# Second half of a 3-D average pool: contiguous loads read two rows at a time, and all stores behind the loads

## The chip, the cores and the metric

The kernel runs on one core of one Trainium2 chip. The metric is the device time of one execution in microseconds, taken as the median of several runs.

## The reference

The input x has the shape (8, 32, 32, 32, 32): batch, channels, depth, height, width, all in float32, 33.5 MB. The output is the mean of every 2 x 2 x 2 window of (depth, height, width), without overlap:

```python
for i, j, k over the output grid (16, 16, 16):
    window = x[:, :, 2*i:2*i+2, 2*j:2*j+2, 2*k:2*k+2]
    result[:, :, i, j, k] = np.mean(window, axis=(-3, -2, -1))
```

The output is float32, 4.2 MB. No element of x is used twice, so the kernel must read 33.5 MB and write 4.2 MB.

## The kernel before

Batch and channels together make 256 rows, each a volume of 32 x 32 x 32 floats, or 128 KB. The kernel takes the rows in two halves of 128, and each row of a half lies on one of the 128 partitions. In the code, `t` is the half and KF = 256 floats (1 KB) is the unit of length along a row: a row is 128 units of input and 16 units of output. One unit of output needs eight units of input, that is two depth slices.

The list `plan` sets the order: for each half, four tiles `tin` of 32 units (32 KB per partition, 4 MB in all) are loaded. The first six tiles are each loaded by one DMA of 4 MB. The last two tiles of the second half are loaded in two parts of 16 units each, 2 MB. In DRAM, neighbouring partitions of such a load lie 128 KB apart. All ten loads are issued by the queue of SyncE (SP) on line 77, in the order of the plan. The pool has five buffers, so the sixth load and the later ones wait until VectorE (DVE) is done with the tile that had the buffer before.

Each tile, or part of one, goes through `pool_unit` on VectorE: line 58 adds the two depth slices (half as many elements come out), line 62 adds neighbours along the width, line 65 adds neighbours along the height, scales by 1/8, and writes the result into `obuf`, one buffer of 16 KB per partition for each half. Line 65 appears in the profile as two instructions, the sum itself and a short one that reads an accumulator which nobody uses.

Four stores on line 92 take the results out, in units of 1 KB per partition: (half 1, units 0 to 1) on the queue of ScalarE (ACT), then on SP (half 0, all 16 units), (half 1, units 2 to 13), and (half 1, units 14 and 15). Since SP takes its instructions in order, its three stores are issued behind the tenth load; the one on ACT is issued as soon as its results are there.

The code after the pool works on the compiled program. It moves the first load in front of the barrier that opens the program, and it rewrites the end, so that SP waits for the stores' semaphores last and everything else is cleared before.

Of the kernel before, what the change touches and what calls it, by code (L numbers as in the profile page):

```python
# [1 line left out]

# [4 lines left out]

F32 = mybir.dt.float32
KF = 256


@with_exitstack
def pool_rows(
    ctx: ExitStack,
    tc: tile.TileContext,
    x: bass.AP,
    kernel_size: int,
    out: bass.AP,
):
    nc = tc.nc  # L20
    assert kernel_size == 2, "only kernel_size == 2 supported"

    B, C, D, H, W = x.shape
    P = nc.NUM_PARTITIONS
    assert (B * C, D, H, W) == (2 * P, 32, 32, 32)
    add = mybir.AluOpType.add

    xv = x.rearrange("b c d h w -> (b c) (d h w)")  # L30
    ov = out.rearrange("b c d h w -> (b c) (d h w)")

    pool_in = ctx.enter_context(tc.tile_pool(name="pin", bufs=5))
    pool_out = ctx.enter_context(tc.tile_pool(name="pout", bufs=1))
    obuf = [pool_out.tile([P, 16 * KF], F32, name=f"obuf{t}") for t in range(2)]
    dummy = pool_out.tile([P, 1], F32, name="dummy")


    plan = [
        (0, 0, (32,)),
        (0, 32, (32,)),
        (0, 64, (32,)),
        (0, 96, (32,)),
        (1, 0, (32,)),
        (1, 32, (32,)),
        (1, 64, (16, 16)),
        (1, 96, (16, 16)),  # L50
    ]

    def pool_unit(buf, t, k0, kb):

        od = kb // 8
        a = buf.rearrange("p (o dd e) -> p o dd e", o=od, dd=2)
        b = buf[:, :od * 1024]
        nc.vector.tensor_add(  # L58
            out=b.rearrange("p (o e) -> p o e", o=od), in0=a[:, :, 0], in1=a[:, :, 1])
        bv = b.rearrange("p (e ww) -> p e ww", ww=2)  # L60
        c = buf[:, od * 1024:od * 1536]
        nc.vector.tensor_add(out=c, in0=bv[:, :, 0], in1=bv[:, :, 1])  # L62
        cv = c.rearrange("p (j hh k) -> p j hh k", hh=2, k=16)
        o0 = k0 * KF // 8
        nc.vector.tensor_tensor_reduce(  # L65
            out=obuf[t][:, o0:o0 + od * 256].rearrange("p (j k) -> p j k", k=16),
            in0=cv[:, :, 0], in1=cv[:, :, 1],
            scale=0.125, scalar=0.0, op0=add, op1=add, accum_out=dummy[:, :],
        )

    for t, k0, parts in plan:
        tin = pool_in.tile([P, 32 * KF], F32, tag="tin", name="tin")
        views = []
        o = 0
        for kb in parts:
            v = tin[:, o * KF:(o + kb) * KF]
            nc.sync.dma_start(  # L77
                out=v, in_=xv[t * P:(t + 1) * P, (k0 + o) * KF:(k0 + o + kb) * KF])
            views.append((v, k0 + o, kb))
            o += kb  # L80
        for v, k, kb in views:
            pool_unit(v, t, k, kb)

    for queue, t, k0, kb in [
        (nc.scalar, 1, 0, 2),
        (nc.sync, 0, 0, 16),
        (nc.sync, 1, 2, 12),
        (nc.sync, 1, 14, 2),  # L90
    ]:
        queue.dma_start(
            out=ov[t * P:(t + 1) * P, k0 * KF:(k0 + kb) * KF],
            in_=obuf[t][:, k0 * KF:(k0 + kb) * KF],
        )


def kernel(tc: tile.TileContext, x: bass.AP, kernel_size: int, out: bass.AP):
    nc = tc.nc
    pool_rows(tc, x, kernel_size, out)  # L100
    tc.close()
    tc.compile()  # L102
    blocks = nc.main_func.blocks

    opening, program = blocks[0].instructions, blocks[tc.starting_block_idx].instructions
    load = next(i for i in program if isinstance(i, mybir.InstDMACopy))
    assert load.engine == nc.sync.engine
    barrier = next(  # L110
        n for n, i in enumerate(opening)
        if i.engine == load.engine and isinstance(i, mybir.InstDrain))
    program.remove(load)
    opening.insert(barrier, load)

    closing = blocks[-1].instructions
    stores = [  # L120
        i for i in program
        if isinstance(i, mybir.InstDMACopy) and "out_" in i.outs[0].memref]
    kept = [u.id for i in stores for u in i.sync_info.on_update]
    kept = [n for j, n in enumerate(kept) if n not in kept[j + 1:]]
    final = next(
        i for i in closing
        if i.engine == nc.sync.engine and isinstance(i, mybir.InstDrain))
    waits = {w.id: w for w in final.sync_info.on_wait}
    closing[closing.index(final)] = mybir.InstDrain(
        name=final.name, engine=final.engine, ins=[], outs=[], is_reset_sema=False,  # L130
        sync_info=mybir.SyncInfo(
            on_wait=[w for n, w in waits.items() if n not in kept], on_update=[]))


    reset = next(
        n for n, i in enumerate(closing)
        if isinstance(i, mybir.InstDrain) and i.is_reset_sema)
    first, stop = closing[reset].reset_range_start, closing[reset].reset_range_stop
    assert isinstance(closing[reset + 1], mybir.InstISA)
    while len(closing) > reset:  # L140
        closing.pop()
    n = first
    while n < stop:
        m = n
        while m < stop and m not in kept:
            m += 1
        if m > n:
            closing.append(mybir.InstDrain(
                name=nc.get_next_instruction_name(), engine=nc.gpsimd.engine, ins=[], outs=[],
                is_reset_sema=True, reset_range_start=n, reset_range_stop=m))  # L150
            nc.gpsimd.sem_clear(range(n, m))
        n = m + 1
    for n in kept:
        w = waits[n]
        closing.append(mybir.InstEventSemaphore(
            name=nc.get_next_instruction_name(), engine=nc.sync.engine, ins=[], outs=[],
            sync_info=mybir.SyncInfo(
                on_wait=[w],
                on_update=[mybir.SyncUpdate(
                    sync_type="semaphore", id=n, ant_name=w.ant_name,  # L160
                    update_mode="sem-sub-imm", update_value=w.wait_value)])))


# [1 line left out]
_INS = ['x', 'kernel_size']  # L165
_OUTS = [((8, 32, 16, 16, 16), 'float32')]

_NUMBERS = {'kernel_size': 2}


# [26 lines left out]
```

## Time and profile before

| | |
|---|---|
| median of 7 runs (lowest to highest) | 91.81 us (91.58 to 92.01) |
| the profiled execution's own time | 92.05 us |
| its span, first to last instruction | 86.8 us |
| VectorE busy | 64.1 us, 40 instructions |
| HBM read, written | 33.55 MB, 4.19 MB |
| share of DMA in the chain that ended last | 83% |

The span ends with the last instruction of VectorE and of the queues; a store that is still under way then is not part of it. The last store is issued at the span's end and takes 4.9 us to land, and the rest of the 92.05 us lies before the first and after the last thing that the trace shows.

In the page, a row of part 2 cuts the span into 40 slices: the digits are the mean busy share of the 16 DMA engines, in tenths. A row of a table of stretches gives a start and an end in microseconds, then its length, the busy time of VectorE and GpSimd in it, the clock, the share of the DMA engines and the GB/s that they moved. A packet is put down to the stretch that it starts in, so short stretches are rough.

### The profile page before, as it was taken

Reading aid. Unit: us, or ns where it says so; the run is one execution under the profiler, and the core shown is the slowest. Engines: PE = TensorE matmul, PEld = TensorE weight load, DVE = VectorE, ACT = ScalarE, POOL = GpSimd, SP = SyncE. Lnnn points to the kernel's source line nnn. Section 1 sums busy time; section 2 is a strip of 40 time slices with the busy share of each in tenths; the row PEclk is TensorE's granted clock in tenths of the full one; section 3 lists DMA queues with packets and bytes.
Section 4 is the critical chain, followed back from the end, with each engine's and each line's share of the span. In section 5 each row is a group of like instructions: output and inputs, shape, how many; then the busy total and the mean of one; then the engine's idle time right before and its main releaser. Section 6 shows DMA issues by size and latency. Waiting matters only on the chain.

```text
span 86.8 us, 91 instructions
## 1 busy us (share of the span) xinstructions
DVE 64.1 (74%) x40; POOL 0.2 (0%) x4
## 2 busy tenths in 40 slices
DVE  0000049992999749992999759992999999999894
POOL 0000000000000000000000000000000000000000
DMA  8979999799998999889997999969999999999999
GB/s 241 423 317 468 483 483 392 332 483 483 468 392 347 483 483 468 362 377 483 483 468 332 408 483 483 453 287 460 383 410 486 419 445 400 460 385 355 445 400 434
DMA packets 1782, 36.58 MB, mean 421 GB/s; under 512 B 192, under 2 KB 192, under 8 KB 320
## 3 DMA queue, kind: packets, MB, share of 16 engines
q1 hardware_dynamic: 1638, 36.32, 98.5%
q10 hardware_dynamic: 144, 0.26, 0.8%
HBM read 33.55 MB, written 4.19 MB: 435 GB/s over the span
## 4 chain that ended last, share of the span: by engine, by line
DMA 83%; DVE 14%; SPq 1%; issue 0%; DVEq 0%
DMA tin<-in_x_dram 83%; DVE tin L58 8%; DVE tin L62 4%; DVE obuf L65 2%; SPq L77 1%; DVE dummy L65 0%; DVEq L102 0%
## 5 line engine op out<-in xcount | busy, mean ns | idle before, releaser
L58 DVE TENSOR_TENSOR tin<-tin 128x4096 f32<-128x4096 f32 (+1 forms) x10 | 35.7, 3569 | 21.0 <-DMA tin<-in_x_dram 21.0
L62 DVE TENSOR_TENSOR tin<-tin 128x2048 f32<-128x2048 f32 (+1 forms) x10 | 18.6, 1865 | 0.3
L65 DVE CUSTOM_DVE_ANT_1 obuf<-tin 128x1024 f32<-128x1024 f32 (+1 forms) x10 | 10.1, 1011 | 0.3
L65 DVE DVE_READ_ACCUMULATOR2_ANT dummy<- 128x1 f32 x10 | 0.8, 81 | 0.0
L178 POOL MEMSET const-uint8-127<- 128x1 uint8 x1 | 0.1, 102 | 0.0
L178 POOL MEMSET const-bfloat16-1.0<- 128x1 bf16 x1 | 0.1, 101 | 0.0
L178 POOL MEMSET const-float32-0.0<- 128x1 f32 x1 | 0.1, 98 | 0.2 <-issue 0.2
L178 POOL MEMSET const-float32-1.0<- 128x1 f32 x1 | 0.1, 98 | 0.0
## 6 DMA issues: line engine op xcount, KB each, us to landing
tin<-in_x_dram SPq DMA_DIRECT2D x6, 4096.0 KB, 35.0
tin<-in_x_dram SPq DMA_DIRECT2D x4, 2048.0 KB, 38.6
out_dram<-obuf SPq DMA_DIRECT2D x1, 2048.0 KB, 37.0
out_dram<-obuf SPq DMA_DIRECT2D x1, 1536.0 KB, 9.1
out_dram<-obuf ACTq DMA_DIRECT2D x1, 256.0 KB, 9.5
out_dram<-obuf SPq DMA_DIRECT2D x1, 256.0 KB, 4.9
```

Of the source, the lines that this page charges most:

```text
L58: nc.vector.tensor_add(out=b.rearrange("p (o e) -> p o e", o=od), in0=a[:, :, 0], in1=a[:, :, 1])
L62: nc.vector.tensor_add(out=c, in0=bv[:, :, 0], in1=bv[:, :, 1])
L65: nc.vector.tensor_tensor_reduce(out=obuf[t][:, o0:o0 + od * 256].rearrange("p (j k) -> p j k", k=16), in0=cv[:, :, 0], in1=cv[:, :, 1], s ...
L77: nc.sync.dma_start(out=v, in_=xv[t * P:(t + 1) * P, (k0 + o) * KF:(k0 + o + kb) * KF])
L178: nc = _bacc.Bacc("TRN2", target_bir_lowering=False, num_devices=1)
```

## The change

In the first half nothing changes but its store. The second half is laid out anew: a load takes a contiguous piece of DRAM, and partition p gets the p-th part of it, instead of part of row p. The four loads of 32, 32, 16 + 16 and 16 + 16 units become four of 24 units and two of 16 units (24 and 16 KB per partition, 3 and 2 MB in all). Since the windows lie within eight units, the pooling of a part stays the same; its result goes to a contiguous piece of the output.

- The compiled program is edited so that a load of the second half names its source as 64 rows of twice the length (48 or 32 KB) and its destination as before, as 128 partitions.
- The first 16-unit part has its depth sum (line 58 before, line 68 after) cut in two instructions of 1024 elements each.
- The store on ACT's queue is gone. The stores are now, all on SP behind the last load: half 1, units 0 to 11 (the 12 KB store, lines 93 to 96); half 0, all 16 units (line 98); half 1, units 12 to 15 (the 4 KB store). On the DRAM side the 12 KB store writes four pieces of 3 KB per partition, and the 4 KB store two of 2 KB. On the SBUF side its source is named as one piece per partition.
- The count that the first store waits for on VectorE is raised by one: it waits not only for the last sum over units 72 to 95, but also for the first of the two halves of the depth sum over units 96 to 111, and so for that load.

In the edited copies a field `ant_dge_precooked` is set to False, which is True in all copies of the kernel before. The five buffers stay.

```diff
-        (1, 0, (32,)),
-        (1, 32, (32,)),
-        (1, 64, (16, 16)),
-        (1, 96, (16, 16)),
+        (1, 0, 24),
+        (1, 24, 24),
+        (1, 48, 24),
+        (1, 72, 24),
+        (1, 96, 16),
+        (1, 112, 16),
...
+        cuts = (0, 1, od) if split else (0, od)
+        for o0, o1 in zip(cuts, cuts[1:]):
+            nc.vector.tensor_add(out=bv[:, o0:o1], in0=a[:, o0:o1, 0], in1=a[:, o0:o1, 1])
...
+        if t == 0:
+            src = xv[:, k * KF:(k + kb) * KF]
+        else:
+            src = xf[P * k * KF:P * (k + kb) * KF].rearrange("(p e) -> p e", p=P)
+        nc.sync.dma_start(out=buf, in_=src)
+        pool_unit(buf, t, k, kb, split=k == 96 and t == 1)
...
-        (nc.scalar, 1, 0, 2),
-        (nc.sync, 0, 0, 16),
-        (nc.sync, 1, 2, 12),
-        (nc.sync, 1, 14, 2),
...
+    for k, n, kb in [(0, 4, 3), (12, 2, 2)]:
+        nc.sync.dma_start(
+            out=of[P * k * KF:P * (k + n * kb) * KF].rearrange("(u p e) -> p u e", u=n, p=P),
+            in_=obuf[1][:, k * KF:(k + n * kb) * KF].rearrange("p (u e) -> p u e", u=n),
         )
+        if k == 0:
+            nc.sync.dma_start(out=ov, in_=obuf[0])
...
+        ap = [list(d) for d in src.ap]
+        row = ap[-1][1]
+        if len(ap) == 3:
+            ap = [ap[0], [1, 1], [1, ap[1][1] * row]]
+        elif "in_" in src.memref and ap[0][0] == row:
+            ap = [[2 * row, 64], [1, 2 * row]]
+        else:
+            continue
+        program[n] = copy.replace(i, ins=[copy.replace(src, ap=ap)], ant_dge_precooked=False)
...
+    waits = [
+        copy.replace(w, wait_value=w.wait_value + 1) if w.ant_name.startswith("DVE") else w
+        for w in store.sync_info.on_wait]
```

## Prediction

> **What bounds the kernel now.** I read the page first, then its chain, then the stretches between landings.
>
> ```profile
> span 86.8 us, 91 instructions
> DVE 64.1 (74%) x40; POOL 0.2 (0%) x4
> ...
> DMA  8979999799998999889997999969999999999999
> ...
> q1 hardware_dynamic: 1638, 36.32, 98.5%
> q10 hardware_dynamic: 144, 0.26, 0.8%
> ...
> DMA tin<-in_x_dram 83%; DVE tin L58 8%; DVE tin L62 4%; DVE obuf L65 2%; SPq L77 1%; DVE dummy L65 0%; DVEq L102 0%
> ```
>
> The reader is to see that the DMA engines are busy throughout (98.5% and 0.8% of their time) and VectorE only 74%. The chain says the same: loads 83%. The time is the sum of what the 16 engines carry, so only fewer or cheaper packets, or a stretch in which they run slowly, can change it. The stretches show how evenly they run:
>
> ```profile
> core 0: us, DVE busy (x) POOL busy (x), PEclk, DMA share, GB/s
> ...
> 40.38:59.78 19.40, 15.90 (x8) 0.00 (x0) 1.00 1.00 432
> ...
> 70.63:75.53 4.90, 4.83 (x7) 0.00 (x0) 1.00 1.00 428
> 75.53:78.10 2.57, 2.54 (x4) 0.00 (x0) 1.00 0.97 414
> 78.10:80.00 1.90, 1.86 (x2) 0.00 (x0) 1.00 1.07 336
> 80.00:81.14 1.14, 1.06 (x3) 0.00 (x0) 1.00 0.91 388
> 81.14:86.00 4.86, 4.22 (x4) 0.00 (x0) 1.00 1.01 434
> ```
>
> The rate is 428 to 434 GB/s except from 78.1 to 80.0, where it is 336 though only the last load runs. In the trace's packet records, two packets of each engine take 0.64 to 1.13 us there instead of 0.61. On its slowest engine the last load takes 5.61 us (75.53 to 81.14), the load before it 4.90 (70.63 to 75.53); on the fastest 5.35. So 0.45 to 0.71 us are lost, right before the first of SP's stores, in the queue since 49.35, begins to move. The end of the kernel:
>
> ```profile
> 81.12 4.99 SPq L92 DMA_DIRECT2D out_dram<-obuf  x2
> 81.46 2.29 DVE L58 TENSOR_TENSOR tin<-tin 128x2048 f32<-128x2048 f32 x1 [0.37 <-DMA tin<-in_x_dram]
> ```
>
> The 12 KB store is issued at 81.12 and the last one at about 85.8. By the packet records the last one's packets start at 88.99 or later, directly behind those of the store before: the engines never run dry, and VectorE's last chain is hidden. The last data packet ends at 90.30, the store lands at 85.76 + 4.9 = 90.66, and 1.39 us up to 92.05 lie outside the trace. The median of the runs shown is 91.81, 0.24 below this execution; I work out differences in its trace and take them from the median.
>
> The packet records give one more price. A packet of 32 KB takes 1213 ns, of 16 KB 611, of 12 KB 460, of 2 KB 84, the 4 byte ones that report completion 9. All fit bytes / 27.2 GB/s + 9 ns: 2048 B are 75 + 9, 32768 B are 1204 + 9.
>
> **What the Trainium skill says.** (1) "DMA: Bandwidth & Descriptors", section "Where 436 GB/s comes from": 16 ports give 435 GB/s. The trace agrees with 432: there is nothing to gain in rate. (2) The same page, "Why small descriptors are slow (HBM only)": an engine pays a fixed overhead of about 3 cycles per packet between its read and write side. The trace agrees that there is a fixed part and measures 9 ns, which I use. (3) The same page, "Why a DMA increments its semaphore by 16 and not by 1": the number of engines is the largest up to 16 that divides both slowest dimensions. For 64 source rows and 128 partitions that is still 16; nothing in the trace of before has unequal sides. The page prices no copy whose reads are longer than its writes. (4) "SBUF — State Buffer", section "Door 1": which four partitions share a port; I need it for one rival only.
>
> **The change part by part.** Bytes stay at 37.7 MB; what changes is packets, order and waits.
>
> *Packets.* Before, an engine has 8 packets per load, 80 in all, and 8 per store, 32: 112, plus 14 completion packets. After, counted by writes: 80 for the loads (ten loads again), 32 + 8 + 16 = 56 for the stores (four pieces of 3 KB, one of 16 KB, two of 2 KB on each of 8 partitions): 136. Counted by reads: 32 + 6 x 4 = 56 for the loads, 8 for each store: 80. Completions: 13. So the bounds are 24 x 9 ns = +0.22 us, if a packet is a write, and 32 x 9 ns = -0.29, if it is a read. Every row of before has equal sides, so the trace can't tell. I take the read side, -0.29: the 9 ns are also what a 4 byte packet takes that moves next to nothing, so they look like the cost of starting a packet, and a long read followed by several writes needs one start.
>
> *The store on ACT's queue leaves the loads.* Its bytes still go out at the end: 0. Interleaving costs nothing now: three loads and this store take 15.28 us (60.25 to 75.53), and their packets add up to 3 x 4.90 + 8 x 84 ns + 9 ns = 15.4. One completion packet less is 0.01.
>
> *Where the loads end.* A 24 KB load has 4 reads of 48 KB: 4 x (1807 + 9) ns + 9 = 7.27 us; a 16 KB load 4 x 1213 ns + 9 = 4.86. From the end of the fourth load (40.84 on the slowest engine): 40.84 + 4 x 7.27 + 2 x 4.86 = 79.64, against 81.14 now.
>
> *VectorE and the added wait.* Durations come from these rows:
>
> ```profile
> L58 DVE TENSOR_TENSOR tin<-tin 128x4096 f32<-128x4096 f32 x6 | 26.5, 4424 | 20.6 <-DMA tin<-in_x_dram 20.6
> L62 DVE TENSOR_TENSOR tin<-tin 128x2048 f32<-128x2048 f32 x6 | 13.7, 2292 | 0.2
> ...
> L65 DVE CUSTOM_DVE_ANT_1 obuf<-tin 128x1024 f32<-128x1024 f32 x6 | 7.3, 1224 | 0.2
> L62 DVE TENSOR_TENSOR tin<-tin 128x1024 f32<-128x1024 f32 x4 | 4.9, 1224 | 0.1
> L65 DVE CUSTOM_DVE_ANT_1 obuf<-tin 128x512 f32<-128x512 f32 x4 | 2.8, 692 | 0.1
> ```
>
> Halfway between them, a part of 24 units takes 3.36 + 1.76 + 0.96 + 0.08 = 6.16 us, less than its load (7.27), so VectorE keeps up. The fourth 24-unit part lands at 41.30 + 4 x 7.27 = 70.4 and is done at 76.5; the third was done at 69.3, so nothing queues. The next part landed at 75.2; its first half sum takes 1.22, so the 12 KB store is issued at 77.8 instead of 76.5: that is the added wait. Behind it on SP are only the 16 KB store, which moves from 49.35 to about 78.3, and the last store, whose data are not ready: the 16-unit part ends at 81.0 (the cut sum costs 2 x 1.22 - 2.29 = 0.16 here, hidden under the stores), the last part at 81.0 + 4.3 = 85.4. No load is behind it; nobody on VectorE waits for a store. With loads ending near 79.7, the stores' 8 x 460 + 8 x 611 ns = 8.6 us carry the engines to 88.3, so the last issue at 85.4 has 2.9 us of cover; without it, each microsecond of delay would cost one. Buffers come free at 55.5 for the last load, which is due at 74.8: 0.
>
> *The slow stretch.* It cost 0.45 to 0.71 us. If a queued store causes it, an issue at 77.8, which reaches the engines 1.0 us later (the first load: issued 0.00, first packet 1.01), leaves it only 0.8 us before the loads end. If it comes with the turn from loads to stores as such, it stays. Bounds: -0.71 and 0. I take about half of 0.5: -0.25.
>
> *The longer issue.* The edited copies have a field of the copy cleared. An issue takes 0.33 to 0.48 us on SP; if it took twice that, nothing changes for the loads (issued 20 us ahead), and the stores have the covers above: 0 to +0.5 us on the first store.
>
> Sum: -0.29 - 0.25 - 0.01, about -0.5: this profile 91.5, the median 91.81 - 0.5 = 91.3.
>
> **The rivals.** (a) *The wide read is cut up again, or writes are what counts*: +0.22 - 0.25, so 91.8 (91.5 to 92.1). For it: each 24 KB still has to be written by a separate write. Against it: nothing but the reason given above.
>
> (b) *The stores come too late* (slower). The store on ACT was issued at 59.06, and its first packet started at 62.69, 3.63 us later, beside busy engines; the first load needed 1.01 on idle ones. In the after kernel no other store is queued, so if the 12 KB store needs 3.63, it starts at 81.4, and the engines idle from 79.6 for 1.8 us; the slow stretch is then gone whole (-0.5) and the reads save 0.29: +1.0, 92.8. It decides from a latency of 79.6 - 77.8 = 1.8 us on, and at 2.6 it has eaten all gains. Against it: ACT's packets had to take turns with another queue's; here the queue is the loads' own.
>
> (c) *Row pairs fall on other engines.* If an engine got eight neighbouring partitions, two engines would, by the port table of (4), write the same port while another idles: half the rate for 16.8 MB, +39 us, about 130. Against it: 64 and 128 rows split in the same proportions.
>
> **How the numbers follow.** Forecast 91.3 (90.9, with the whole slow stretch gone, to 91.6, with none): 47%. (a) 25%, (b) 24% (91.9 to 92.9), (c) 4%. A difference under 0.2%, 0.18 us, can't be told from none here. Faster: 45 + 9 = 54%; within: 2 + 10 + 3 = 15%; slower: 6 + 21 + 4 = 31%. The range 90.9 to 92.5 leaves out (c), half of (b) and a little at the low end, 20%.
>
> **What would show it.** Packets of 48 KB at 1.81 us and 32 KB at 1.21 in the second half, and an unchanged cost of the stores, prove the read side; packets of 24 KB at 0.91 and 3 KB at 0.12 prove (a). The last load should end near 79.7 to 79.9 and no stretch from 60 to 88 fall under 400 GB/s; a gap in DMA between 79.6 and 81.5 is (b). The forecast is wrong if the 9 ns follow the writes, or if the last issue comes after about 87.

## The result, and the profile after

The changed kernel takes 91.41 us (median of 12 runs, 91.27 to 91.54), the kernel before 91.86 us in the same comparison (31 runs, 91.52 to 92.21). The ratio is 0.9953, with a 95% interval from 0.9942 to 0.9965: 0.45 us or 0.5% faster. The forecast was 91.3. The sum was nearly right, but two of its terms were not, and by luck they made up for each other.

The stretches first, over the same times as before (start and end in us, length, busy time of VectorE and GpSimd, clock, DMA share, GB/s), from the changed kernel's trace:

```profile
core 0: us, DVE busy (x) POOL busy (x), PEclk, DMA share, GB/s
...
70.63:75.53 4.90, 4.83 (x3) 0.00 (x0) 1.00 1.00 428
75.53:78.10 2.57, 2.54 (x4) 0.00 (x0) 1.00 0.95 408
78.10:80.00 1.90, 1.86 (x2) 0.00 (x0) 1.00 1.03 433
80.00:81.14 1.14, 1.11 (x4) 0.00 (x0) 1.00 0.97 410
81.14:86.00 4.86, 3.83 (x4) 0.00 (x0) 1.00 1.02 432
```

The slow stretch (336 GB/s from 78.1 to 80.0) is gone: 433. By the packet records the last load takes 4.89 us on the slowest engine (74.69 to 79.58), as long as the load before it, where it took 5.61 in the kernel before.

The page's line of DMA packets and its part 6 (size and median time from issue to landing), first from the kernel before, then from the changed kernel:

```profile
DMA packets 1782, 36.58 MB, mean 421 GB/s; under 512 B 192, under 2 KB 192, under 8 KB 320
...
out_dram<-obuf SPq DMA_DIRECT2D x1, 2048.0 KB, 37.0
```

```profile
DMA packets 1297, 36.72 MB, mean 424 GB/s; under 512 B 176, under 2 KB 176, under 8 KB 176
...
tin<-in_x_dram SPq DMA_DIRECT2D x4, 3072.0 KB, 34.5
tin<-in_x_dram SPq DMA_DIRECT2D x2, 2048.0 KB, 25.4
out_dram<-obuf SPq DMA_DIRECT2D x1, 2048.0 KB, 10.3
out_dram<-obuf SPq DMA_DIRECT2D x1, 1536.0 KB, 6.1
out_dram<-obuf SPq DMA_DIRECT2D x1, 512.0 KB, 4.8
```

There are fewer packets than the 1782 of before: a packet is a read, so the wide reads do what the edit says. The 16 KB store (2048 KB in all) now lands 10.3 us after its issue, not 37.0: it no longer waits long in the queue. But the records show what the wide packets cost (the most frequent time of each kind):

| packet | time | over its bytes at 27.22 GB/s |
|---|---|---|
| load, 32 KB, one write (first half) | 1213 ns | 9 ns |
| load, 48 KB, two writes | 1829 ns | 23 ns |
| load, 32 KB, two writes | 1227 ns | 23 ns |
| store, 12 KB, four writes | 466 ns | 15 ns |
| store, 4 KB, two writes | 159 ns | 9 ns |

So a load packet with two writes takes 23 ns over its bytes. At 9 ns for each packet with one write, two of those would take 18; but run 11, which keeps the layout and reads narrow, has packets of 24 KB that take 915 ns in the mean, 12 over their bytes, so that two of them take as much as a wide one. These times aren't spent one after another in full: an engine's next packet starts 3 to 4 ns before the record of the one before it ends. From start to start, a packet of 32 KB with one write takes 1209 ns, 5 to 6 over its bytes, and one of 48 KB with two writes 1824, about 19 over. The issues at the end, from the timeline:

```profile
77.61 0.62 SPq L93 DMA_DIRECT2D out_dram<-obuf  x1
78.28 0.58 SPq L98 DMA_DIRECT2D out_dram<-obuf  x1
...
85.06 0.57 SPq L93 DMA_DIRECT2D out_dram<-obuf  x1
```

The first store's packets start at 79.12, where the first engine ends its loads, and the last store's run directly behind the 16 KB store's (88.2 on the slowest engine). So the engines never run dry. The last store lands at 85.06 + 4.8 = 89.9, and this execution's own time is 91.27.

### The profile page after: what moved, and what is told of

The parts are those of the page before. It is cut to its first block, busy times and chain, and to the rows that moved or that the text cites. A ratio compares the mean times of both kernels' runs of the same rounds, so it can differ in the third digit from the quotient of the medians.

```text
span 86.6 us, 91 instructions
## 1 busy us (share of the span) xinstructions
DVE 64.5 (74%) x41; POOL 0.2 (0%) x4
## 4 chain that ended last, share of the span: by engine, by line
DMA 70%; DVE 26%; issue 0%; SPq 0%; DVEq 0%
DMA tin<-in_x_dram 70%; DVE tin L68 14%; DVE tin L71 8%; DVE obuf L74 4%; SPq L87 0%; DVE dummy L74 0%; DVEq L105 0%
## 5 line engine op out<-in xcount | busy, mean ns | idle before, releaser
L68 DVE TENSOR_TENSOR tin<-tin 128x4096 f32<-128x4096 f32 (+3 forms) x11 | 35.9, 3260 | 19.9 <-DMA tin<-in_x_dram 19.9
L71 DVE TENSOR_TENSOR tin<-tin 128x2048 f32<-128x2048 f32 (+2 forms) x10 | 18.7, 1865 | 0.3
L74 DVE CUSTOM_DVE_ANT_1 obuf<-tin 128x1024 f32<-128x1024 f32 (+2 forms) x10 | 10.1, 1011 | 0.3
## 6 DMA issues: line engine op xcount, KB each, us to landing
out_dram<-obuf SPq DMA_DIRECT2D x1, 2048.0 KB, 10.3
```

What stands on the lines that cost most here:

```text
L68: nc.vector.tensor_add(out=bv[:, o0:o1], in0=a[:, o0:o1, 0], in1=a[:, o0:o1, 1])
L74: nc.vector.tensor_tensor_reduce(out=obuf[t][:, o0:o0 + od * 256].rearrange("p (j k) -> p j k", k=16), in0=cv[:, :, 0], in1=cv[:, :, 1], s ...
```

## The experiments

The theory after the result (A, and in later runs L): the gain is the slow stretch, and the slow stretch comes from a store that was queued long before the loads ended; wide reads, the layout and the added wait bring nothing. The rivals: the wide reads (B) or the contiguous loads (C2) gain; or the slow stretch belongs to the old layout, the old order or the store on ACT's queue (C), or to the turn from loads to stores and the kind of store that comes first (S). Each ratio is to runs of the kernel before on the same chip (medians 91.77 to 91.88).

**1. Narrow reads.**

```diff
-        elif "in_" in src.memref and ap[0][0] == row:
-            ap = [[2 * row, 64], [1, 2 * row]]
```

> The changed kernel, but its second-half loads keep 128 source rows of 24 or 16 KB; layout, order, stores and the added wait stay. Theory A (the wide reads bring nothing: in the changed kernel's trace a read of 48 KB takes 1829 ns, 23 over its bytes, and two packets of 24 KB would take 2 x 9 over theirs): 6 loads x 4 x 5 ns less, 91.3 us, at most 91.4. Rival B (the wide reads bring part of the gain of 0.45): 91.6 or more.

Measured: 91.36 us, ratio 0.9962 (0.9950 to 0.9974). The wide reads bring nothing. By the packet records the 16 KB loads take 4.86 us each instead of 4.89, but the 24 KB loads are no shorter: from the end of the fourth load to the end of the tenth, the changed kernel takes 38.97 to 38.98 us (on the first and on the last engine to end), this run 38.97 to 39.21, and run 11, narrow too, 38.98. The expected 0.12 isn't there.

**2. No added wait.**

```diff
-        copy.replace(w, wait_value=w.wait_value + 1) if w.ant_name.startswith("DVE") else w
+        copy.replace(w, wait_value=w.wait_value + 0) if w.ant_name.startswith("DVE") else w
```

> The changed kernel without the added wait: the 12 KB store, and the 16 KB store behind it, are issued at about 76.4 instead of 77.6, with the loads' packets ending at 79.6. Theory A (stores queued behind the last load slow its packets, as from 78.1 to 80.0 in the kernel before): the slow stretch comes back at least in part, 91.5 to 91.9. Rival C (the slow stretch belonged to the old order or to the old layout): 91.4 as the changed kernel.

Measured: 91.37 us, 0.9959 (0.9947 to 0.9971). The two stores' issues, and the stretch that was slow:

```profile
76.69 0.63 SPq L93 DMA_DIRECT2D out_dram<-obuf  x1
77.37 0.58 SPq L98 DMA_DIRECT2D out_dram<-obuf  x1
```

```profile
78.10:80.00 1.90, 1.87 (x2) 0.00 (x0) 1.00 0.99 420
```

The added wait brings nothing, and a store that is queued 3 us before the loads end does no harm. Theory A expected some here; it had the lead time wrong.

**3. The 16 KB store first, queued at once.** The added wait is off, as in run 2; so it is in runs 7, 8, 10, 11 and 12.

```diff
+    nc.sync.dma_start(out=ov, in_=obuf[0])
     for k, n, kb in [(0, 4, 3), (12, 2, 2)]:
...
-        if k == 0:
-            nc.sync.dma_start(out=ov, in_=obuf[0])
```

> The changed kernel with the 16 KB store in front, so that it is queued behind the loads from about 55.6 on; the 12 KB store follows at 76.4, without the added wait. Theory A: the slow stretch is back whole, 0.45 to 0.7 us: 91.9 to 92.1, as the kernel before. Rival C (the old layout of the loads, or the store on ACT's queue, made it): 91.4.

Measured: 91.95 us, 1.0016 (1.0008 to 1.0025): the whole gain is lost by one store that is first and queued early. Its timeline and its stretches:

```profile
55.83 0.58 SPq L92 DMA_DIRECT2D out_dram<-obuf  x1
76.61 9.16 SPq L94 DMA_DIRECT2D out_dram<-obuf  x2
```

```profile
75.53:78.10 2.57, 2.50 (x5) 0.00 (x0) 1.00 0.96 408
78.10:80.00 1.90, 1.87 (x2) 0.00 (x0) 1.00 1.03 362
80.00:81.14 1.14, 1.10 (x4) 0.00 (x0) 1.00 1.04 446
```

The slow stretch is back (362), again in the packets of the last load: all but one of the slow ones start at 78.12 to 78.50, and they take up to 1829 ns instead of 1227, while the store's first packet starts at 79.63. Neither the old layout nor a store on ACT's queue is there, so neither is needed for it.

**4. A later first store.** The wait of run 2's diff, raised by 2 in place of 1.

> The changed kernel, its first store waiting for one more VectorE instruction: issued at about 78.85 instead of 77.6. In the changed kernel the store's first packet comes directly behind the loads, 1.5 us after its issue, so its latency is 1.5 us at most. If it is 1.5, the packets start at 80.35 and the engines idle 0.8 us: 92.2. If it is 1.0, as for the first load, they idle 0.3: 91.7. The rival of the forecast with 3.63 us would give 94.

Measured: 92.21 us, 1.0053 (1.0041 to 1.0065). The first store's issue and the stretches show the engines running dry:

```profile
79.02 0.62 SPq L93 DMA_DIRECT2D out_dram<-obuf  x1
```

```profile
75.53:78.10 2.57, 2.50 (x5) 0.00 (x0) 1.00 0.98 421
78.10:80.00 1.90, 1.86 (x2) 0.00 (x0) 1.00 0.61 259
80.00:81.14 1.14, 1.11 (x4) 0.00 (x0) 1.00 0.83 345
```

Here the DMA share falls to 0.61, while in run 3's slow stretch it stays at 1.03. A share over so short a stretch is rough, and the packet records decide: here the loads ended at 79.24 to 79.74 and the store's first packet started at 80.30, so each engine stood idle for 0.5 us or more; in run 3's slow stretch the packets follow each other with hardly a pause (0.2 us in all, summed over the 16 engines). The store was issued at 79.02, 1.28 us before its first packet. Of that, 0.62 is the issue on SP itself (the edited copies' longer issue); from its end to the first packet are 0.66 us, much as for the first load (1.01 - 0.38 = 0.63). So the mechanism of the slower rival is real, and its price is 0.8 us for an issue that is 1.41 us later. The changed kernel escapes it by 79.12 - 77.61 - 1.28 = 0.23 us.

**5. Narrow stores.**

```diff
-        if len(ap) == 3:
-            ap = [ap[0], [1, 1], [1, ap[1][1] * row]]
-        elif "in_" in src.memref and ap[0][0] == row:
+        if "in_" in src.memref and ap[0][0] == row:
```

> The changed kernel, but the sources of the 12 KB and the 4 KB store are named in pieces of 3 and 2 KB as their destinations are. If a store's packet is a read, as the changed kernel's records show (12 KB packets of 466 ns), this makes 32 and 16 packets per engine of 122 and 84 ns, of 8 and 8 of 466 and 160: +0.17 and +0.06, 91.6. If the engine joins the pieces by itself, 91.4.

Measured: 91.58 us, 0.9972 (0.9962 to 0.9982); packets of 3 KB take 121 ns and of 2 KB 84, and the 12 KB store holds the slowest engine for 3.90 us instead of 3.70. For stores too the packet is the read, and cutting reads up costs: 0.17 us here, against an expected 0.23.

**6. The kernel before with late stores** (its layout, loads and ACT store kept).

```diff
-        (nc.sync, 0, 0, 16),
-        (nc.sync, 1, 2, 12),
-        (nc.sync, 1, 14, 2),
+        (nc.sync, 1, 2, 10),
+        (nc.sync, 0, 0, 16),
+        (nc.sync, 1, 12, 4),
```

> The kernel before with its own layout and loads, and its store on ACT's queue; only SP's stores are cut and ordered anew: units 2 to 11 of half 1 first (10 KB, issued at 76.8, when the last load still has 3.7 us to go), then the 16 KB store, then units 12 to 15. Theory L (the last load is slowed by a store that was queued long before the loads end): the slow stretch goes, 91.3 to 91.4. Rival C (the layout of the loads makes it): 91.8. Rival S (any store with writes of 10 KB and more, behind the last load, makes it): 91.8.

Measured: 91.69 us, 0.9984 (0.9974 to 0.9994), between all expectations. The last load took 5.11 us on the slowest engine, not 5.61, and not 4.90. Part of the gain comes; run 9 takes the store on ACT's queue away as well.

**7. The 16 KB store first, but late.** Run 3, with this store given the wait of the next one:

```diff
-        on_wait=waits, on_update=store.sync_info.on_update))
+        on_wait=list(second.sync_info.on_wait), on_update=store.sync_info.on_update))
```

> As the run with the 16 KB store in front, but that store too waits for the sum that the 12 KB store waits for, so both are issued at 76.4 instead of 55.6 and 76.6. Theory L (long queueing is the cause): no slow stretch, 91.4. Rival S (the 16 KB store, with one write of 16 KB per read, directly behind the last load is the cause, whenever it is issued): 91.9 to 92.0.

Measured: 91.44 us, 0.9963 (0.9952 to 0.9975). Runs 3 and 7 have the same packets in the same order on the queue. Only the issue of one store differs, 55.83 or 76.64 (and that of the next, behind it, by 0.4), and with it 0.5 us:

```profile
76.64 0.35 SPq L92 DMA_DIRECT2D out_dram<-obuf  x1
77.04 8.74 SPq L94 DMA_DIRECT2D out_dram<-obuf  x2
```

```profile
75.53:78.10 2.57, 2.50 (x5) 0.00 (x0) 1.00 1.01 434
78.10:80.00 1.90, 1.86 (x2) 0.00 (x0) 1.00 0.94 397
80.00:81.14 1.14, 1.11 (x4) 0.00 (x0) 1.00 1.07 460
```

A packet counts where it starts, so 397 and 460 are one rate cut at a bad place: 421 over both. By the records three of the last load's 64 packets are still slow (up to 1362 ns), where run 3 has 16. The turn from loads to stores as such, and which store is first, do next to no harm.

**8. The 16 KB store first and early, in writes of 4 KB.** Run 3, with the destination of that store named in pieces:

```diff
+        outs=[copy.replace(dst, ap=[[4096, 128], [1024, 4], [1, 1024]])],
```

> As the run with the 16 KB store in front, queued from 55.6 on, but its destination is named as four pieces of 4 KB, with one read of 16 KB. Theory L: slow stretch as there, 91.9 to 92.0. Rival S (large writes): no slow stretch, 91.4.

Measured: 92.03 us, 1.0025 (1.0015 to 1.0035). The size of the waiting store's writes doesn't matter.

**9. The old layout with the new order of stores.**

```diff
-        (nc.scalar, 1, 0, 2),
-        (nc.sync, 0, 0, 16),
-        (nc.sync, 1, 2, 12),
-        (nc.sync, 1, 14, 2),
+        (nc.sync, 1, 0, 12),
+        (nc.sync, 0, 0, 16),
+        (nc.sync, 1, 12, 4),
```

> The kernel before with its own layout, its loads and no wide reads; only the stores are those of the changed kernel in size, queue and order (12, 16 and 4 KB, all on SP, the first one issued at 76.8 to 77.1), and none is among the loads. Theory L plus the store on ACT's queue (the run with late stores that kept it stood at 91.69, and its last load still took 0.2 too long): the whole gain without the new layout, 91.3 to 91.4. Rival C2 (contiguous loads are worth the remaining 0.3 us): 91.7 as in that run.

Measured: 91.46 us, 0.9970 (0.9955 to 0.9986). That is 0.35 us below the kernel before on its chip, where the changed kernel was 0.45 below, and the two intervals overlap: a few lines about stores bring most of the gain, and the rest can't be told from none, without the new layout, wide reads, added wait or any edited copy. The last load takes 4.94 us. Much of what this execution (91.66) loses against the changed kernel's, it loses elsewhere: its fourth and fifth loads take 9.83 us in the median over the engines, where those of the kernel before take 9.68 and 9.69.

**10. The 16 KB store first, at a middle time.** Run 7 with an earlier sum to wait for:

```diff
-        on_wait=list(second.sync_info.on_wait), on_update=store.sync_info.on_update))
+        on_wait=[copy.replace(w, wait_value=21) for w in second.sync_info.on_wait],
+        on_update=store.sync_info.on_update))
```

> As the run with the 16 KB store in front and late, but it waits for an earlier sum and is issued at about 69.1, 10.6 us before the loads end and before the last load's first packet (74.3 to 74.7), not after it (76.6). Theory L with the order of the packets (what counts is whether the store is queued before the last load has begun): the slow stretch is back, 91.8 to 92.0. Theory L with time (the harm needs a wait of tens of us): 91.4 to 91.6.

Measured: 91.92 us, 1.0016 (1.0009 to 1.0023), and the slow stretch:

```profile
69.30 0.35 SPq L92 DMA_DIRECT2D out_dram<-obuf  x1
76.60 9.15 SPq L94 DMA_DIRECT2D out_dram<-obuf  x2
```

```profile
75.53:78.10 2.57, 2.50 (x5) 0.00 (x0) 1.00 1.01 408
78.10:80.00 1.90, 1.87 (x2) 0.00 (x0) 1.00 0.90 310
80.00:81.14 1.14, 1.10 (x4) 0.00 (x0) 1.00 1.04 446
```

Queued 10 us ahead, the store costs as much as 24 us ahead; 3 us ahead it costs next to nothing. Between 69.30 and 76.64 lies the start of the last load's packets (74.4 to 74.8).

**11. Narrow reads and no added wait**: the diffs of 1 and 2 together.

> The changed kernel without the wide reads of its loads and without the added wait. Each alone changed nothing; both away should stand at 91.3 to 91.4 as well. If one covered for the other, 91.6 or more.

Measured: 91.36 us, 0.9957 (0.9944 to 0.9970). Neither covered for the other. It is a simpler kernel at the same time as the changed one; none of the runs is faster than it beyond the intervals.

**12. A store among the loads again.** Run 2, with part of its first store on ACT's queue:

```diff
+    nc.scalar.dma_start(
+        out=of[:P * 3 * KF].rearrange("(p e) -> p e", p=P), in_=obuf[1][:, :3 * KF])
-    for k, n, kb in [(0, 4, 3), (12, 2, 2)]:
+    for k, n, kb in [(3, 3, 3), (12, 2, 2)]:
```

> The changed kernel without the added wait (91.37 as a run), but the first 3 units of half 1 go out on ACT's queue at about 55.1, among the loads, as such a store did in the kernel before; SP's first store then has 9 KB. Theory as predicted (a store among the loads costs only its own packets, which the end no longer has): 91.4. Rival (a store among the loads slows them, or spreads the engines, and its removal is part of the gain of 0.45): 91.6.

Measured: 91.36 us, 0.9937 (0.9923 to 0.9950). A store among the loads costs only its own packets, which the end no longer has. The Trainium skill, "DMA: Bandwidth & Descriptors", section "Issuing engines are not separate DMA queues", says that all queues run on the same 16 engines and interleave; the trace agrees, with ACT's packets of 3 KB lying between those of loads from 58.7 to 72.0. The run is also a warning about short stretches:

```profile
78.10:80.00 1.90, 1.83 (x3) 0.00 (x0) 1.00 0.76 328
80.00:81.14 1.14, 1.13 (x1) 0.00 (x0) 1.00 0.79 332
```

This looks like a slow or idle end and is neither. With each packet counted for the part of it that lies in the stretch, the records give 429 and 426 GB/s here, with all 16 engines busy; the same count gives 320 for the slow stretch of the kernel before, 351 in run 3, 339 in run 10, and 426 in the changed kernel, so those readings stand.

## Why the prediction was right, and which steps failed

- *The bound: right.* The engines are the bound before and after; VectorE's 64.5 us stay hidden, and so does the cut sum.
- *The slow stretch: right in kind, too small.* The step took half of 0.5 us, -0.25, for the case that a queued store causes it and a shorter lead only shrinks it. Runs 3, 7 and 10 show that a queued store does cause it, and that with a lead of 3 us it is gone, but for a trace: 91.95 and 91.92 against 91.44, so -0.5 us. One reading beside it was loose: the rate isn't "428 to 434 GB/s except from 78.1 to 80.0", as the table shown there has 414 and 388 on both sides. With packets counted by the part in the stretch these are 430 and 412, so the slow packets do sit where the text put them.
- *The packets: this step failed.* "I take the read side, -0.29." A packet is a read, for loads and stores (table, run 5), but a saved packet saved no time. For the loads, 4 x 7.27 + 2 x 4.86 = 38.80 us were forecast from the fourth load's end on; they took 38.98, and 38.98 in run 11 with twice as many packets. Two things were wrong in the term. First, 9 ns is the excess of a record and not of time: a packet's record overlaps the next one's by 3 to 4 ns, and from start to start a packet with one write takes 5 to 6 ns over its bytes. Second, a long read with two writes isn't as cheap as one start: 19 ns from start to start, as much as the two narrow packets of run 11 (9 each). The stores' packets take 9.81 to 9.89 us per engine, where the four stores of before took 9.8. Over the whole end, from the fourth load's end to the last packet, the changed trace is 0.47 to 0.60 us shorter, and the slow stretch alone was 0.45 to 0.71. So the term measures between 0 and +0.1 in place of -0.29. The inference from the 4 byte packet (a packet's cost is that of its start) was wrong for loads. The fixed cost per packet that the Trainium skill, "DMA: Bandwidth & Descriptors", section "Why small descriptors are slow (HBM only)", speaks of is there, at 5 to 6 ns, but neither it nor the trace of before said what a second write adds. Why a narrow packet costs 9 in run 11 and 5 to 6 in the first half is open.
- *The sum.* About -0.5 and 0 to +0.1 us make -0.4 to -0.5, against 0.45 measured and 0.55 forecast. The forecast is near because one term was 0.25 too small and the other 0.3 to 0.4 too large. That is luck, and the time alone would not have told.
- *The added wait and the covers: right in place.* Predicted issues 77.8 and 85.4, measured 77.61 and 85.06, in an execution whose fourth load ended 0.24 us earlier. The cover of the last store held. That of the first was only 0.23 us, which the text did not see, since it weighed the chance of a late start and not the margin. What the longer issue added (0.62 us instead of 0.33 to 0.48) came out of this cover, so it didn't reach the time.
- *The rival with late stores: its mechanism is real, its price of 3.63 us is not.* On the loads' own queue the latency is 1.28 us (run 4), of which 0.62 is the issue.
- *The store on ACT's queue costing nothing: right* (run 12). *Row pairs on other engines: did not happen*, the wide loads run on all 16 engines, four packets each, at 428 GB/s.

What stays open is how a store that waits in the queue slows the load in front of it. The runs show when (issued before the last load's packets start, not after), how much (0.5 us) and where (in packets of the last load that start 1 to 3 us before the store's first packet), and that the writes' size has no part in it. They don't separate a lead of time from the place among the packets. Run 6, with a store on ACT's queue, kept 0.2 us of the stretch although its stores on SP were issued late; its interval overlaps that of run 9, so whether that is more than chance is open too. In run 12, with such a store as well, the last load took 5.10 us on its slowest engine, at no cost in time.

## What to carry to other kernels

When the DMA engines are the bound, compare the rate of stretch after stretch, and where it dips look at the packets: long packets with hardly a pause between them are a slow transfer, a pause is a late issue, and neither means that the stretch was cut at a bad place (run 12). A store that is ready early isn't best issued early: here, behind the loads on the same queue, it cost 0.5 us, and issued 3 us before the loads' end nothing, while by run 4's latency an issue less than 1.28 us before their end leaves the engines idle. Price a packet from start to start and not by its record, and a new form of transfer from both sides, reads and writes, before counting its packets as a gain.

## What was not expected of the hardware

- A load packet with two writes took 23 ns over its bytes; one with one write 9 ns in the first half and 12 in run 11's second half; a store packet of 12 KB with four writes 15 ns, with one write 9.
- Packets of one engine overlap by 3 to 4 ns in the records.
- A store queued 10 to 24 us ahead slowed the last load in front of it by 0.55 to 0.8 us on the slowest engine (5.44, 5.60 and 5.71 us in runs 3, 10 and 8, against 4.89).
- The changed kernel's 12 runs spread over 0.27 us, the 31 runs of the kernel before over 0.69; more runs spread wider by chance alone.
- The copies with the edited field took 0.62 us on SP for the 12 KB store; the 16 KB store, which isn't edited, took 0.35 in run 7, but 0.58 in the changed kernel, directly behind an edited one.
